# HGRN2 in a hybrid decoder trunk: the two pairs of heads in one run of small products

## The chip, the cores and the metric

The kernel runs on one core of one Trainium2 chip, in float32 throughout. The metric is device time in microseconds (us), as the median of several runs. One more execution was recorded with the hardware profiler; all rows of a profile come from such an execution.

## The reference

Two layers; in each a SwiGLU half step, three token mixers side by side on the same normalised input, an output projection, and another SwiGLU half step, on 512 tokens of width 1024. The change concerns one mixer, HGRN2: four heads of width 64, a gated linear recurrence, in chunks of 64 tokens.

```python
log_f = log_sigmoid(z) + log1p(lb * exp(-z))         # per token and channel
k = (1 - lb) * sigmoid(-z)

def step(state, inp):                                # one chunk of 64 tokens
    qb, kb, vb, lfb = inp
    bcum = cumsum(lfb, axis=-2)
    rel = bcum[..., :, None, :] - bcum[..., None, :, :]
    decay = where(causal, exp(where(causal, rel, 0)), 0)
    scores = einsum('bhtd,bhsd,bhtsd->bhts', qb, kb, decay)
    o = einsum('bhts,bhsv->bhtv', scores, vb) + einsum('bhtd,bhdv->bhtv', qb * exp(bcum), state)
    b_last = bcum[..., -1:, :]
    state = exp(b_last)[..., 0, :, None] * state + einsum('bhsd,bhsv->bhdv', kb * exp(b_last - bcum), vb)
    return state, o

o = rms_norm(o, out_gain) * silu(gate)
```

## The kernel before

Nearly all of the time goes into large dense products: 128x128 weights against 512 or 256 columns. Each float32 factor is split into a rounded part and a rest (ScalarE casts, VectorE subtracts, lines 435 and 438 for weights that come by DMA), and a product is three matmuls. A *granule* is one load of weight rows with its products; in the projections of the FoX mixer (`fox_qkv`, through `tokens`, line 536) a granule is 24 matmuls of 512 columns in four banks of the PSUM ("mm" three times and "po"), and its generator stops after each half, so that other work can be put between half granules of 12. Three such projections of four granules follow each other (first half of q and k, second half, v). When one is complete, ScalarE copies its four banks out (line 1696), and the next one uses the same banks.

HGRN2 works on two *pairs* of heads, two heads of 64 channels on the 128 partitions. `hgrn` is a generator, one for each pair, and stops at these places: after the decays; after the scaled keys; after their transposes (line 1426); after the state products U (line 1448), the scan over chunks and the operands of the first two levels; after each of four groups of score levels; after the outputs (lines 1577 and 1593); the end normalises.

The scores of a chunk, 64 by 64, are made level by level. Level n splits the chunk in blocks of 2^n tokens; within a block, queries of the second half meet keys of the first, with a decay relative to the middle. `operands(lev)` makes exp of the relative decay for keys and queries on VectorE and ScalarE (lines 1487, 1488, the exponential, 1495), `score(lev, ...)` multiplies on TensorE (line 1510 for levels 0 and 1, line 1518 for levels 2 to 6), `place` (lines 1530, 1535, 1538) takes the valid part from the bank into the matrix A under a mask. The groups are levels 0 and 1, 2 and 3, 4 and 5, and 6. All these products are small: 64x64 weights in a quarter of the array, with 32 or 64 columns, or 128x64 weights with 2 columns; each is recorded as two matmuls.

`mix` steps the two generators in turn and puts half granules of the dense projection behind each step, after the list `HGRN_BESIDE`: none behind the first steps of both, one behind each of the next six, two behind each of the next six, one behind each of the last two that have any. So on TensorE a run of small products of the first pair, dense work, a run of the second pair, dense work, and so on. `fox_decay` (line 1634) comes after the eighth step.

Dense products marked with `follow` keep the order in which they are written. The rest is ordered by the framework's scheduler when the program is built: by the order of the code, among what its own estimate of times takes to be ready; casts of weights have priority. Each engine then executes its queue in order. Temporary tiles of 128x512 come from a ring of ten (`tmp`). PSUM has eight banks: "mm" three, "sc" two, "pt" two, "po" one, each tag used in rotation; accesses to a bank by different engines are kept apart bank by bank. Before, U takes two "pt" banks for each pair, and the scores one or two "sc" banks for each pair and group.

Of the kernel before, what the change touches and what calls it, by code (L numbers as in the profile page):

```python
# [21 lines left out]
QUADS = ((("mm", 0), ("mm", 1), ("mm", 2), ("po", 0)), (("sc", 0), ("sc", 1), ("pt", 0), ("pt", 1)))  # L22

LEVELS = ((0, 1), (2, 3), (4, 5), (6,))
HGRN_BESIDE = (0, 0) + (1,) * 6 + (2,) * 6 + (1,) * 2

BESIDE = (3, 3, 1) + (1, 1, 1, 1, 1, 2, 2) + (1, 2, 2, 2, 2, 2, 1, 2, 2)
P = 128
T = 512
# [171 lines left out]
def halves(x):  # L201

    return x.rearrange("p (h t) -> p h t", h=2)
# [7 lines left out]
class Trunk:  # L211
# [944 lines left out]
    def mix(self, l, w, w_out, conv_w, out_gain, q_gain, k_gain, f_bias, next_gain, logits):  # L1156
# [3 lines left out]
        with tc.tile_pool(name=self.n("mix"), bufs=1) as mp:  # L1160
# [48 lines left out]
            with tc.tile_pool(name=self.n("hg"), bufs=1) as hp:  # L1209
                self.tt, self.tb = "t", 10  # L1210

                b, kb, q, S = (pair(mp, tag) for tag in ("b", "kb", "q", "S"))
                negc = mp.tile([NH, 2, T], F32R, tag="n", name=self.n("negc"))
                bz = features([(H_F, 256)], ("mm", "mm"), lambda: self.end_norm(self.bank("pt"), hp))
                if l == 0:
                    self.lower_bounds(logits, hp.tile([P, T], F32, tag="t", name=self.n("lb"), bufs=10))
                bg = features([(H_G, 256)], ("mm", "po"))
                inv = self.inv
                z, sg = pair(hp, "z"), pair(hp, "sg")
                for i in range(2):  # L1220
                    nc.vector.tensor_mul(halves(z[i]), unwoven(bz[i]), halves(inv))
                for i in range(2):
                    nc.vector.tensor_mul(halves(sg[i]), unwoven(bg[i]), halves(inv))
                self.table(SILU)
                for i in range(2):
                    self.act(sg[i], sg[i], AF.Silu)
                self.table(LNEXP)

                self.invc, self.inv2 = col("invc", 4), col("inv2", 4)
                row = self.dram.tile([1, T], F32, tag="row", name=self.n("row"))  # L1230
                nc.gpsimd.dma_start(row, inv[0:1, :])
                nc.gpsimd.dma_start(self.invc, row.rearrange("o (i p) -> (o p) i", p=P))
                nc.vector.scalar_tensor_tensor(
                    out=self.inv2, in0=self.invc, scalar=1.0 / HD, in1=self.invc,
                    op0=ALU.mult, op1=ALU.mult,
                )
                bq = features([(H_Q, 256)], ("mm", "mm"))
                for i in range(2):
                    nc.vector.tensor_mul(halves(q[i]), unwoven(bq[i]), halves(inv))

                bv = [self.bank(t) for t in ("mm", "sc", "sc", "po")]
                self.stream(
                    [(bv[i][:, :264], slice(0, 264), TOK[i]) for i in range(4)],
                    cols((H_I, 128), (F_F, 4), (H_I + 128, 128), (F_F + 4, 4)), self.xact, KD,
                )
                v = hp.tile([P, 4, 256], F32, tag="v", name=self.n("v"))
                zf = mp.tile([P, 4, NH], F32, tag="zf", name=self.n("zf"))
                for i in range(4):
                    nc.scalar.activation(
                        halves(v[:, i, :]), unwoven(bv[i][:, :256]), AF.Copy,  # L1250
                        scale=self.invc[:, i : i + 1],
                    )
                    nc.vector.scalar_tensor_tensor(  # L1253
                        out=halves(zf[:, i, :]), in0=unwoven(bv[i][:, 256:264]),
                        scalar=self.invc[:, i : i + 1], in1=halves(fb), op0=ALU.mult, op1=ALU.add,
                    )
                run = [
                    self.hgrn(l, pr, hp, z[pr], q[pr], v, sg[pr], og, S[pr], kb[pr], b[pr])
                    for pr in range(2)
                ]  # L1260
                half = []
                dense = self.fox_qkv(mp, hp, tokens, half)
                step = 0
                while run:
                    for g in list(run):
                        if next(g, "end") == "end":
                            run.remove(g)
                        step += 1
                        for _ in range(HGRN_BESIDE[step - 1] if step <= len(HGRN_BESIDE) else 0):
                            next(dense)  # L1270
                        if step == 8:
                            self.fox_decay(mp, hp, zf, negc)
            with tc.tile_pool(name=self.n("at"), bufs=1) as ap_:
                self.tt, self.tb = "t", 2
                attend = self.fox_attend(ap_, half, qkg)
# [101 lines left out]
        nc.vector.tensor_sub(self.yl[i], u, self.yh[i])  # L1377


    def hgrn(self, l, pr, hp, z, q, v, sg, og, S, kb, b):  # L1380

# [5 lines left out]
        tmp = lambda: hp.tile([P, T], F32, tag="t", name=self.n("t"), bufs=self.tb)  # L1389
        own = lambda tag, shape: hp.tile(shape, F32, tag=f"{tag}{pr}", name=self.n(tag))  # L1390
        lb, lb1 = self.lb[:, l, pr : pr + 1], self.lb1[:, l, pr : pr + 1]

        h, t, n = tmp(), tmp(), tmp()
        nc.vector.tensor_scalar(h, z, scalar1=0.0, scalar2=0.5, op0=ALU.min, op1=ALU.mult)
# [45 lines left out]

        U, dec, S = tmp(), tmp(), S.rearrange("p (v c) -> p v c", c=NCH)
        U3, dec3 = (a.rearrange("p (v c) -> p v c", c=NCH) for a in (U, dec))
        ub = [self.bank("pt") for _ in range(2)]
        for i in range(4):
            for par, hh in ((0, 0), (1, 1), (0, 1), (1, 0)):
                r = slice(CH * par, CH * par + CH)
                o = slice(64 * hh, 64 * hh + 64)
                nc.tensor.matmul(
                    ub[par][o, i * HD : (i + 1) * HD],
                    kt[r, i * P + 64 * hh : i * P + 64 * hh + 64],  # L1450
                    v[r, i, pr * P + 64 * hh : pr * P + 64 * hh + 64], start=True, stop=True,
                )
        for par in range(2):
            nc.scalar.copy(
                U3[:, :, par::2], ub[par][:, :256].rearrange("p (i v) -> p v i", i=4)
            )
# [14 lines left out]
        def operands(lev):  # L1471
            w, half = 2**lev // 2, halves(lev)
            e = tmp()
            if lev == 0:

                nc.vector.tensor_mul(e, q, k)
                return e
            if lev == 1:
                self.act(half(e, 1), half(lf, 1), AF.Exp)
                nc.vector.tensor_mul(half(e, 1), half(e, 1), half(q, 1))  # L1480
                nc.vector.tensor_mul(half(e, 0), half(e, 1), half(k, 0))
                return e
            n2 = T // (2 * w)
            ref = b.rearrange("p (n s) -> p n s", s=2 * w)[:, :, w - 1 : w].to_broadcast(
                [P, n2, w]
            )
            nc.vector.tensor_add(half(e, 0), half(kb, 0), ref)
            nc.vector.tensor_sub(half(e, 1), half(b, 1), ref)
            self.act(e, e, AF.Exp)
            if len(asked) % 2 == 0:  # L1490
                asked.append(tmp())
            else:
                asked.append(asked[-1])
            e2 = asked[-1][:, (len(asked) - 1) % 2 * (T // 2) :][:, : T // 2]
            nc.vector.tensor_mul(
                e2.rearrange("p (n w) -> p n w", w=w), half(e, 1), half(q, 1)
            )
            return e, e2


        asked = []

        def score(lev, e, sb, at):

            if lev > 1:
                e, e2 = e
            if lev < 2:
                for c in range(NCH):
                    r = slice(CH * (c % 2), CH * (c % 2) + CH)
                    nc.tensor.matmul(  # L1510
                        sb[0][r, 8 * at + c // 2 : 8 * at + 8 : 4], e[:, c * CH : (c + 1) * CH],
                        self.heads2, start=True, stop=True,
                    )
                return
            for i in range(4):
                for hh, par in ((0, 0), (1, 1), (0, 1), (1, 0)):
                    r, c = slice(64 * hh, 64 * hh + 64), 2 * i + par
                    nc.tensor.matmul(
                        sb[hh][CH * par : CH * par + CH, P * at + 32 * i : P * at + 32 * i + 32],
                        e[r, c * CH : (c + 1) * CH], e2[r, 32 * c : 32 * c + 32],  # L1520
                        start=True, stop=True,
                    )

# [23 lines left out]
        yield  # L1547
        for g, levels in enumerate(LEVELS):
            now, ready = ready, []
            asked.clear()  # L1550
            later = list(LEVELS[g + 1]) if g + 1 < len(LEVELS) else []
            sb = [self.bank("sc") for _ in range(2 if g else 1)]
            for at, lev in enumerate(levels):
                score(lev, now[at], sb, at)
            for at, lev in enumerate(levels):
                if later:
                    ready.append(operands(later.pop(0)))
# [441 lines left out]
```

## Time and profile before

| | |
|---|---|
| median of 3 runs | 1761.5 us (1760.98 to 1762.36) |
| the profiled execution, time | 1760.3 us |
| the profiled execution, span of the records | 1758.5 us |
| granted TensorE clock | 1.00 |
| TensorE matmuls busy | 1749.8 us, 13613 records |
| VectorE busy | 1410.7 us |
| ScalarE busy | 1009.7 us |

In the rows, PE is TensorE's matmuls, PEld its weight loads, DVE VectorE, ACT ScalarE, SP the engine that issues most DMAs. A row of a timeline has its start from the beginning of the span and its length, both in us, then engine, line, operation, output and inputs, shape and how many in a row; in brackets, idle time before it and what ended it. L451, L457, L458 and L536 are dense products.

### The profile page before, as it was taken

The numbers are of one execution on the slowest core, as the hardware profiler recorded it, in microseconds if no ns is written. First come the engines' busy times: TensorE is split into PE (matmuls) and PEld (weight loads), VectorE is DVE, ScalarE is ACT, GpSimd is POOL, SyncE is SP. The second block draws the span as 40 slices with busy tenths as digits, with TensorE's granted clock in tenths as the row PEclk, the third lists the DMA queues.
The fourth block names the chain that finished last, engine by engine and source line by source line (L and its number), as shares of the span: only waits on it lengthen the run. The fifth ranks groups of instructions, "written<-read, shape, count | busy, mean of one in ns | idle before, by whom it ended". The sixth has DMA issues, their size and how long they took to land.

```text
span 1758.5 us, 33346 instructions
## 1 busy us (share of the span) xinstructions
PE 1749.8 (100%) x13613; PEld 1644.2 (93%) x13613; DVE 1410.7 (80%) x1898; ACT 1009.7 (57%) x1397; POOL 177.2 (10%) x174
## 2 busy tenths in 40 slices
PE   9999999999999999999999999999999999999999
PEld 7999999888888899999989999998888889999998
DVE  7988788678777898888689887876778779888793
ACT  5565555465776565565446556555657655655652
POOL 0011120100000111112001111201000000120200
PEclk9999999999999999999999999999999999999999
DMA  7768784243543876868267787923435438687762
GB/s 203 187 144 198 181 178 110 73 125 88 138 119 98 214 169 155 204 168 172 84 187 168 178 185 175 190 76 79 120 95 141 115 109 215 156 180 192 162 139 96
DMA packets 257465, 262.34 MB, mean 149 GB/s; under 512 B 25832, under 2 KB 236528, under 8 KB 257312
## 3 DMA queue, kind: packets, MB, share of 16 engines
q1 hardware_dynamic: 201456, 192.02, 36.4%
q0 software_dynamic: 55840, 68.19, 24.1%
q8 instruction: 107, 1.75, 0.4%
q14 instruction: 46, 0.38, 0.1%
q10 hardware_dynamic: 16, 0.00, 0.0%
HBM read 226.15 MB, written 2.17 MB: 130 GB/s over the span
## 4 chain that ended last, share of the span: by engine, by line
PE 92%; DVE 5%; ACT 1%; issue 1%; DMA 1%; SPq 0%; ACTq 0%; DVEq 0%
PE mm L451 10%; PE mm L458 10%; PE mm L457 10%; PE mm L536 8%; PE sc L458 6%; PE sc L451 6%; PE sc L457 6%; PE pt L457 6%; PE pt L451 6%; PE pt L458 6%; PE po L451 3%; PE po L457 3%; PE po L458 3%; PE po L536 2%; PE sc L1767 1%; DVE hl L438 1%
## 5 line engine op out<-in xcount | busy, mean ns | idle before, releaser
L940 DVE TENSOR_TENSOR hl<-w,hl 128x1024 fp32r<-128x1024 f32 x279 | 340.7, 1223 | 90.1 <-ACT hl L938 88.4
L938 ACT CAST hl<-w 128x1024 fp32r<-128x1024 f32 x279 | 292.7, 1049 | 198.3 <-PE mm L458 56.0
L438 DVE TENSOR_TENSOR hl<-st,hl 128x1024 fp32r<-128x1024 f32 (+3 forms) x152 | 159.9, 1053 | 100.9 <-ACT hl L435 100.1
L435 ACT CAST hl<-st 128x1024 fp32r<-128x1024 f32 (+3 forms) x151 | 137.5, 911 | 158.2 <-PE po L458 44.4
L451 PE MATMUL mm<-xc,hl 128*128 128x256 f32 x698 | 191.6, 275 | 0.1
L458 PE MATMUL mm<-xc,hl 128*128 128x256 f32 x696 | 191.6, 275 | 0.0
L457 PE MATMUL mm<-xc,hl 128*128 128x256 f32 x696 | 191.5, 275 | 0.0
L451 PE MATMUL pt<-xc,hl 128*128 128x256 f32 x546 | 149.7, 275 | 0.0
L457 PE MATMUL pt<-xc,hl 128*128 128x256 f32 x544 | 149.7, 275 | 0.0
L458 PE MATMUL pt<-xc,hl 128*128 128x256 f32 x544 | 149.6, 275 | 0.0
L451 PEld LDWEIGHTS mm<-xc,hl 128*128 128x128 f32 x698 | 133.9, 192 | 0.3 <-ACT u L1058 0.3
L458 PEld LDWEIGHTS mm<-xc,hl 128*128 128x128 f32 x696 | 133.6, 192 | 0.4 <-DVE hl L940 0.4
L457 PEld LDWEIGHTS mm<-xc,hl 128*128 128x128 f32 x696 | 133.6, 192 | 0.0
L458 PE MATMUL sc<-xc,hl 128*128 128x256 f32 x464 | 127.8, 275 | 0.1
L451 PE MATMUL sc<-xc,hl 128*128 128x256 f32 (+1 forms) x466 | 127.7, 275 | 0.0
L457 PE MATMUL sc<-xc,hl 128*128 128x256 f32 x464 | 127.7, 275 | 0.0
L536 PE MATMUL mm<-hl,x 128*128 128x512 f32 x432 | 108.3, 386 | 0.4 <-DVE zf L1253 0.4
L451 PE MATMUL mm<-x,hl 128*128 128x512 f32 x272 | 105.4, 388 | 0.0
L451 PEld LDWEIGHTS pt<-xc,hl 128*128 128x128 f32 x546 | 104.7, 192 | 0.0
L457 PEld LDWEIGHTS pt<-xc,hl 128*128 128x128 f32 x544 | 104.4, 192 | 0.0
L458 PEld LDWEIGHTS pt<-xc,hl 128*128 128x128 f32 x544 | 104.4, 192 | 0.0
L458 PE MATMUL mm<-x,hl 128*128 128x512 f32 x272 | 103.1, 379 | 0.0
(524 smaller groups left out, 5454.6 us busy)
## 6 DMA issues: line engine op xcount, KB each, us to landing
w<-in_ffn_w_in_dram SPq DMA_DIRECT2D x124, 512.0 KB, 6.3
w<-in_ffn_w_out_dram POOLq DMA_DIRECT2D x50, 512.0 KB, 9.6
w<-in_ffn_w_out_dram SPq DMA_DIRECT2D x49, 512.0 KB, 4.7
st<-in_ffn_w_out_dram SPq DMA_DIRECT2D x39, 512.0 KB, 3.7
st<-in_w_mix_in_dram SPq DMA_DIRECT2D x72, 256.0 KB, 3.0
st<-in_ffn_w_in_dram SPq DMA_DIRECT2D x70, 256.0 KB, 3.9
w<-in_ffn_w_in_dram POOLq DMA_DIRECT2D x29, 512.0 KB, 10.0
w<-S POOLq DMA_DIRECT2D x29, 512.0 KB, 5.1
```

Source lines behind the costliest of these rows:

```text
L435: a = nc.scalar.copy(hi, src[:, c : c + w])
L438: b = nc.vector.tensor_sub(lo, src[:, c : c + w], hi)
L451: i = nc.tensor.matmul(acc[:, c], ah, bh[:, c.start // 2 : c.stop // 2, :], start=first and c.start == 0, stop=False, skip_group_check=True,)
L457: nc.tensor.matmul(acc, ah, bl, start=False, stop=False, skip_group_check=True)
L458: i = nc.tensor.matmul(acc, al, bh, start=False, stop=last, skip_group_check=True)
L536: self.follow("p", self.nc.tensor.matmul(acc, *((w, woven(x)) if toks is None else (x[:, toks], woven(w))), start=k == 0 and id(acc) not i ...
L938: A(nc.scalar.copy(hi, src))
L940: return lambda: V(nc.vector.tensor_sub(lo, src, hi))
L1767: mm = lambda *a, **k: E(nc.tensor.matmul(*a, skip_group_check=True, **k))
```

## The change

The two generators are stepped together from the U products on. Each has two more stops: after the U products, and after the score products of each group. So the small products of both pairs are issued one behind the other, then both pairs' evictions and next operands, then the half granules that stood behind each pair before: 2, 4, 4, 4 and 2. The first three steps alternate as before, with the same half granules; `fox_decay` comes after the first joint step.

The pairs share banks: a table `both` holds the banks of a group, and each pair has half of their 512 columns. The groups alternate between the "sc" and the "pt" banks.

The product of the relative decay with q is written in place, into the half of the operand tile that holds the queries' decay, instead of into a packed tile of its own (`e2`, `asked`); the score products read it there, in pieces of 2^(lev-1) columns.

```diff
-HGRN_BESIDE = (0, 0) + (1,) * 6 + (2,) * 6 + (1,) * 2
+HGRN_BESIDE = (0, 0, 1, 1, 1, 1), (2, 4, 4, 4, 2)
...
+                both = {}
                 run = [
-                    self.hgrn(l, pr, hp, z[pr], q[pr], v, sg[pr], og, S[pr], kb[pr], b[pr])
+                    self.hgrn(l, pr, hp, z[pr], q[pr], v, sg[pr], og, S[pr], kb[pr], b[pr], both)
                     for pr in range(2)
                 ]
...
-                step = 0
-                while run:
-                    for g in list(run):
-                        if next(g, "end") == "end":
-                            run.remove(g)
-                        step += 1
-                        for _ in range(HGRN_BESIDE[step - 1] if step <= len(HGRN_BESIDE) else 0):
-                            next(dense)
-                        if step == 8:
-                            self.fox_decay(mp, hp, zf, negc)
+                alone, together = HGRN_BESIDE
+                for step, n in enumerate(alone):
+                    next(run[step % 2])
+                    for _ in range(n):
+                        next(dense)
+                for step, n in enumerate(together):
+                    for g in run + run:
+                        next(g)
+                    for _ in range(n):
+                        next(dense)
+                    if step == 0:
+                        self.fox_decay(mp, hp, zf, negc)
+                for g in run:
+                    next(g)
+                for g in run:
+                    assert next(g, "end") == "end"
...
+        def shared(key, *tags):
+            if key not in both:
+                both[key] = [self.bank(tag) for tag in tags]
+            return [b[:, pr * T // 2 : (pr + 1) * T // 2] for b in both[key]]
...
-        ub = [self.bank("pt") for _ in range(2)]
+        ub = shared("u", "pt", "pt")
         for i in range(4):
...
+        yield
         for par in range(2):
             nc.scalar.copy(
...
-            if len(asked) % 2 == 0:
-                asked.append(tmp())
-            else:
-                asked.append(asked[-1])
-            e2 = asked[-1][:, (len(asked) - 1) % 2 * (T // 2) :][:, : T // 2]
-            nc.vector.tensor_mul(
-                e2.rearrange("p (n w) -> p n w", w=w), half(e, 1), half(q, 1)
-            )
-            return e, e2
+            nc.vector.tensor_mul(half(e, 1), half(e, 1), half(q, 1))
+            return e
...
+                    keys = e[r, c * CH : (c + 1) * CH]
+                    out = sb[hh][CH * par : CH * par + CH, P * at + 32 * i : P * at + 32 * i + 32]
                     nc.tensor.matmul(
-                        sb[hh][CH * par : CH * par + CH, P * at + 32 * i : P * at + 32 * i + 32],
-                        e[r, c * CH : (c + 1) * CH], e2[r, 32 * c : 32 * c + 32],
+                        out.rearrange("p (n w) -> p n w", w=2**lev // 2), keys, halves(lev)(keys, 1),
                         start=True, stop=True,
                     )
...
-            sb = [self.bank("sc") for _ in range(2 if g else 1)]
+            sb = shared(g, *(("pt", "sc")[g % 2 == 0],) * (2 if g else 1))
             for at, lev in enumerate(levels):
                 score(lev, now[at], sb, at)
+            yield
             for at, lev in enumerate(levels):
                 if later:
                     ready.append(operands(later.pop(0)))
```

More of the change, by code (lines that the diff above doesn't have):

```diff
@@ L1377, in conv_out, with hgrn @@
         nc.vector.tensor_sub(self.yl[i], u, self.yh[i])
-    def hgrn(self, l, pr, hp, z, q, v, sg, og, S, kb, b):
+    def hgrn(self, l, pr, hp, z, q, v, sg, og, S, kb, b, both):
         nc = self.nc
@@ L1489, in operands @@
             self.act(e, e, AF.Exp)
-            if len(asked) % 2 == 0:
-                asked.append(tmp())
-            else:
-                asked.append(asked[-1])
-            e2 = asked[-1][:, (len(asked) - 1) % 2 * (T // 2) :][:, : T // 2]
-            nc.vector.tensor_mul(
-                e2.rearrange("p (n w) -> p n w", w=w), half(e, 1), half(q, 1)
-            )
-            return e, e2
-        asked = []
+            nc.vector.tensor_mul(half(e, 1), half(e, 1), half(q, 1))
+            return e
         def score(lev, e, sb, at):
-            if lev > 1:
-                e, e2 = e
             if lev < 2:
@@ L1549, in hgrn @@
             now, ready = ready, []
-            asked.clear()
             later = list(LEVELS[g + 1]) if g + 1 < len(LEVELS) else []
-            sb = [self.bank("sc") for _ in range(2 if g else 1)]
+            sb = shared(g, *(("pt", "sc")[g % 2 == 0],) * (2 if g else 1))
             for at, lev in enumerate(levels):
                 score(lev, now[at], sb, at)
+            yield
             for at, lev in enumerate(levels):
```

## The prediction, made before the change was run

> **What bounds the kernel now.** I read the page first: the busy times, then the chain that ended last.
>
> ```profile
> PE 1749.8 (100%) x13613; PEld 1644.2 (93%) x13613; DVE 1410.7 (80%) x1898; ACT 1009.7 (57%) x1397; POOL 177.2 (10%) x174
> ...
> PE 92%; DVE 5%; ACT 1%; issue 1%; DMA 1%; SPq 0%; ACTq 0%; DVEq 0%
> ```
>
> TensorE (PE) works for the whole span and carries 92% of the chain, so time changes only by what happens on PE's own timeline. The change touches the HGRN2 part of each layer. The PE timeline places it, in the first layer, from the transposes near 381 us to the outputs that begin near 441 us; the second layer does the same about 868 us later. The windows view gives each engine's load there, for both layers, and then for two stretches of the first.
>
> ```profile
> 387.00:441.00 54.00, 54.00 (x654) 44.56 (x656) 44.19 (x97) 29.09 (x51) 1.04 (x2) 1.00 0.32 89
> 1255.00:1309.00 54.00, 54.00 (x651) 44.55 (x649) 44.26 (x97) 29.03 (x51) 1.04 (x2) 1.00 0.32 91
> ```
> ```profile
> 394.00:408.00 14.00, 14.00 (x121) 11.48 (x120) 12.78 (x24) 10.27 (x19) 0.00 (x0) 1.00 0.30 75
> 408.00:421.00 13.00, 13.00 (x178) 10.96 (x176) 12.90 (x35) 5.46 (x10) 0.52 (x1) 1.00 0.29 85
> ```
>
> After the stretch and its length come PE, weight loads, VectorE (DVE), ScalarE (ACT) and GpSimd, then the granted clock (1.00). The layers agree within 0.1 us on every engine, so I work out one and double it. PE has no hole. DVE is close behind it: 12.78 of 14 us, then 12.90 of 13. That is the second thing to watch: PE can only be brought forward as far as DVE delivers operands.
>
> What can be saved on a PE that is never idle? Only the turn between kinds of products, so the PE timeline comes next. Its columns are start, length of the group, and what it is. L536 is the dense stream (128x128 weights, 512 columns), L1518 the score products (64x64 weights, 32 columns). A product has two records.
>
> ```profile
> 412.04 1.46 PE L536 MATMUL mm<-hl,x 128*128 128x512 f32 x6
> 413.34 0.59 PE L536 MATMUL po<-hl,x 128*128 128x512 f32 x2
> ...
> 420.86 0.38 PE L536 MATMUL po<-hl,x 128*128 128x512 f32 x1
> 421.17 1.14 PE L1518 MATMUL sc<-t,t 64*64 64x32 f32 x64
> 422.23 3.72 PE L536 MATMUL mm<-hl,x 128*128 128x512 f32 x16
> 425.79 1.03 PE L536 MATMUL po<-hl,x 128*128 128x512 f32 x4
> ```
>
> Undisturbed, six dense records take 413.34 - 412.04 = 1.30 us, 0.217 each. The last dense record before the small run starts at 420.86 and its slot ends at 421.08; the next dense one starts at 422.23. So 64 small records hold the stream up for 1.15 us. The sixteen dense ones behind them take 425.79 - 422.23 = 3.56 us where 16 x 0.217 = 3.47 would do: another 0.09. A run of 64 costs 1.24 us in all. The last score level has runs of 32:
>
> ```profile
> 433.53 0.59 PE L536 MATMUL po<-hl,x 128*128 128x512 f32 x2
> 434.05 0.67 PE L1518 MATMUL sc<-t,t 64*64 64x32 f32 x32
> 434.65 1.56 PE L536 MATMUL mm<-hl,x 128*128 128x512 f32 x6
> ...
> 437.13 0.38 PE L536 MATMUL po<-hl,x 128*128 128x512 f32 x1
> 437.44 0.76 PE L1518 MATMUL sc<-t,t 64*64 64x32 f32 x32
> 438.13 1.56 PE L536 MATMUL mm<-hl,x 128*128 128x512 f32 x6
> ```
>
> The first: 434.65 - 433.53 - 2 x 0.217 = 0.69, with the 0.09 behind it 0.78. The second: 438.13 - 437.13 - 0.217 = 0.78, so 0.87. From 32 to 64 records the cost rises by 1.24 - 0.78 = 0.46 us; doing nothing but turning in and out costs 0.78 - 0.46 = **0.32 us per run**, however long the run. That is what the change goes after.
>
> **The change part by part.** *Pairs in one run.* Per layer the first pair's run and the second pair's become one, for the state products (U), the two lowest levels, levels 2 and 3, levels 4 and 5, and level 6. The outputs already follow each other without dense work between, and stay so. No product is added or removed, and the count of dense half granules is the same (20, with 2+4+4+4+2 behind the merged runs where it was 1+1, 2+2, 2+2, 2+2, 1+1). For the U and low-level runs the rows are:
>
> ```profile
> 387.27 0.69 PE L1448 MATMUL pt<-v,t 64*64 64x64 f32 x32
> ...
> 395.33 1.10 PE L1510 MATMUL sc<-heads,t 128*64 128x2 f32 x32
> ...
> 401.21 0.59 PE L536 MATMUL po<-hl,x 128*128 128x512 f32 x2
> 401.74 1.10 PE L1510 MATMUL sc<-heads,t 128*64 128x2 f32 x32
> 402.77 3.72 PE L536 MATMUL mm<-hl,x 128*128 128x512 f32 x16
> 406.36 1.13 PE L536 MATMUL po<-hl,x 128*128 128x512 f32 x4
> ```
>
> A U run of 32 lasts 0.69 against 0.67 for the score run of 32: I give it the same 0.32. The low-level run costs 402.77 - 401.21 - 2 x 0.217 + 0.09 = 1.22 us. The groups of the page's fifth part give one record's own time, 199 ns:
>
> ```profile
> L1510 PE MATMUL sc<-heads,t 128*64 128x2 f32 x128 | 4.4, 199 | 0.0
> ```
>
> So the 32 start within 1.10 - 0.20 = 0.90 us, 0.029 apart, 32 of them are 0.93 and the turn is 0.29. The merged level 6 is a run of 64: 1.24 instead of 0.78 + 0.87, a gain of 0.41; if the second run's extra 0.09 comes along, 0.32. Sum per layer: 0.32 + 0.29 + 0.32 + 0.32 + 0.41 = 1.66 us, twice 3.3 us; with the lower value for level 6, 3.2.
>
> *Operands in place.* The score products read their 32 moving columns straight out of the 64-column tile, in pieces of 2 to 32, where they read them closely packed. No row shows such a read. [...] The U row has 64 columns and takes 0.02 us more per 32 records than the 32-column row; 640 records (5 levels, 2 pairs, 16 products, 2 records, 2 layers) make 20 x 0.02 = 0.4 us. A gain has no row to speak for it: U shows that columns aren't what limits these runs. I take 0. [...]
>
> On DVE the product with q now lands strided and in place instead of packed. The nearest rows are these: L1481 writes strided in place, L1495 packed.
>
> ```profile
> 396.60 0.57 DVE L1481 TENSOR_TENSOR t<-t,lk 128x256 f32<-128x256 f32 x1
> ...
> 406.79 0.41 DVE L1495 TENSOR_TENSOR t<-t,q 128x256 f32<-128x256 f32 x1
> ```
>
> At most 0.16 us more for each of ten per layer, 1.6 us on DVE, not on PE's path as long as operands come early; at best nothing. I take nothing. One temporary tile less per stage loosens the ring of ten.
>
> *Shared banks.* Evictions of the first pair now wait for the second's products in the same bank, 0.93 us more. Queued behind them on DVE are the next levels' operands. Hidden: the next merged run comes four half granules later, 4 x 12 x 0.217 = 10.4 us.
>
> *The second pair earlier.* This is the price. Its level-1 operand is wanted three times 16 records after the run begins, at 395.33 - 0.32 = 395.01, plus 3 x 16 x 0.029 = 396.4; in the trace it was ready at 396.60 + 0.57 = 397.2. Its level-3 operand was ready at 406.79 + 0.41 = 407.2 and is wanted when the granules behind the low levels end, at 395.01 + 2 x 0.93 + 0.09 + 10.4 = 407.4 or a little later. The first is late by 0.8 us unless DVE reaches it sooner. I think it does: the ACT timeline shows what held the second pair back.
>
> ```profile
> 392.55 1.06 ACT L1564 COPY lk<-S 128x448 f32<-128x448 f32 x1 [2.47 <-DVE t L1481]
> 393.51 0.76 ACT L1454 COPY t<-pt 128x256 f32<-128x256 f32 x2
> ...
> 400.18 1.04 ACT L1696 COPY qk<-mm 128x512 f32<-128x512 f32 x2
> ...
> 405.20 0.63 ACT L341 ACTIVATE t<-t 128x512 f32<-128x512 f32 x1
> 405.73 0.57 ACT L1696 COPY qk<-po 128x512 f32<-128x512 f32 x1
> ```
>
> The second pair's U copies (393.51) stood behind a copy that waited 2.47 us for the first pair. With both U products done near 387.27 + 0.69 + 0.46 = 388.4 they need not, and the second scan, which followed them, can start some 2 us sooner. I cost the earlier pair at nothing, covered by those 2 us; without that cover it costs 0.8 us per layer.
>
> Against the profiled execution (1760.3 us, 1.2 below the median of 1761.5) the sum gives 1757.0; against the median, **1758.2 us**.
>
> **The rivals.** *Late second pair.* DVE, 98% busy, keeps its old times: PE waits 0.8 us at the low levels in each layer, the rest has margin. Gain 3.3 - 1.6 = 1.7: 1759.8 us. For it: the DVE load. Against it: the freed 2 us.
>
> *Not merged.* Instructions without a written order are placed by the framework's scheduler as they become ready. Where it sees the second pair's operands late, dense halves go in between and the runs stay apart: no gain, 1761.5 us. Against it: the old runs stayed whole, and from levels 2 and 3 on margins are microseconds.
>
> *The banks of the projection.* This is the slower one. Its four banks are reused at once by the next projection. So far the second pair's low-level run stood between (1.22 us); now nothing does. ACT empties them, in order. The first two copies began at 400.18, in front of the second pair's exponential of level 3 (405.20 to 405.83). Issued earlier in the code now, that exponential can come ahead of them in ACT's queue and hold them: first bank free at 405.83 + 0.52 = 406.35. PE wants it when the projection ends, at 401.21 + 2 x 0.217 + 0.93 - 0.32 = 402.3. It would stand for about 4.1 us per layer: 1761.5 - 3.3 + 8.2 = 1766.4 us. It turns the gain into a loss when the first copy ends after 402.3 + 1.66 = 404.0. Against it: the exponential itself would come sooner than 405.20, with its operands. [...] In this trace evacuation stays ahead of PE.
>
> **How the numbers follow.** Forecast (merged, no new wait) 0.56; late second pair 0.16; not merged 0.13; banks 0.12; the rest 0.03. The forecast's own spread is 1757.5 to 1758.9: the 0.4 us of strided reads, the level-6 term, and small waits that go or come. The range 1757.0 to 1762.0 takes in the second and third case with the scatter of the medians and leaves out the banks and the rest, about 0.15, and the tails. About what a measurement of this kernel can tell from no change is 0.2%, 3.5 us: the boundaries are 1758.0 and 1765.0. The forecast lies almost on the first, so a bit under half of it, with a little of the rest, counts as faster: 0.30. Slower is the bank case less its mild forms: 0.10. The same: 0.60.
>
> **What would show it.** In the new PE timeline: one run of 64 records for U, the low levels and level 6, 128 for the others, about 1.24 + 2 x 0.46 = 2.16 us of held-up stream for 128, and no gap but the turn. Wrong steps would show as: a dense group between two L1518 groups of one stage (not merged); the last quarter of L1510 starting late behind DVE (late pair); the second projection's first dense group late behind ACT L1696 (banks); L1518 records further apart than 0.46 / 32 = 0.0144 us (strided reads). The forecast is wrong if the turn isn't the fixed cost I read from runs of two lengths.

## The result, and the profile after

The changed kernel took 1757.95 us (median of 21 runs), the kernel before 1760.65 us (21 runs). The ratio is 0.9986, 95% interval 0.998 to 0.9993: by the ratio 2.5 us less, between 1.2 and 3.5. The interval lies below 1, so the kernel is faster, but by less than the 3.3 us of the sum; by the boundary of 0.2% that the prediction set, it counts as the same, the case to which it gave 0.60. The predicted 1758.2 us looks closer than it was: it started from 1761.5, a median of three runs, 0.85 us above the median of 21, and that hides that the gain came out smaller; the closeness is luck. One execution of the kernel before, beside e1 to e4 below, took 3022.98 us at a mean granted clock of 0.556; it is in no ratio here.

The profiled execution took 1757.89 us against 1760.3. The page's first lines:

```profile
span 1756.1 us, 33330 instructions
...
PE 1748.3 (100%) x13613; PEld 1645.5 (94%) x13613; DVE 1409.4 (80%) x1898; ACT 1010.5 (58%) x1397; POOL 177.0 (10%) x174
```

As many products as before, PE still full. The PE timeline of the first layer, at the places shown of before (U is now line 1461, the low levels 1512, the other levels 1522):

```profile
387.24 0.38 PE L536 MATMUL po<-hl,x 128*128 128x512 f32 x1
387.55 1.16 PE L1461 MATMUL pt<-v,t 64*64 64x64 f32 x64
388.64 1.56 PE L536 MATMUL mm<-hl,x 128*128 128x512 f32 x6
...
395.17 2.03 PE L1512 MATMUL sc<-heads,t 128*64 128x2 f32 x64
397.13 3.72 PE L536 MATMUL mm<-hl,x 128*128 128x512 f32 x16
...
402.42 3.68 PE L536 MATMUL mm<-hl,x 128*128 128x512 f32 x16
406.40 1.13 PE L536 MATMUL po<-hl,x 128*128 128x512 f32 x4 [0.30 <-ACT qk L1699]
407.37 0.59 PE L536 MATMUL mm<-hl,x 128*128 128x512 f32 x2
407.80 0.59 PE L536 MATMUL po<-hl,x 128*128 128x512 f32 x2
408.32 2.07 PE L1522 MATMUL pt<-t 64*64 64x32 f32 x128
410.32 1.56 PE L536 MATMUL mm<-hl,x 128*128 128x512 f32 x6
...
432.91 0.59 PE L536 MATMUL po<-hl,x 128*128 128x512 f32 x2
433.44 1.14 PE L1522 MATMUL pt<-t 64*64 64x32 f32 x64
434.50 1.56 PE L536 MATMUL mm<-hl,x 128*128 128x512 f32 x6
```

All five pairs of runs are merged (levels 4 and 5, not among the lines shown, have their 128 records from 420.88 on). A run of 128 holds the dense stream up for 410.32 - 407.80 - 2 x 0.217 = 2.09 us, 2.18 with what the dense records behind it lose. The same arithmetic on the starts of all dense records gives the gain by stage, per layer: U 0.36, low levels 0.38, levels 2 and 3 0.33, levels 4 and 5 0.33, level 6 0.42, together 1.81 us.

Not all of it was kept. Between 402.42 and 406.40 sixteen dense records of the second projection take 3.98 us instead of 3.47, and the four behind them 0.97 instead of 0.87: 0.61 us, 0.63 by the single records, where it was 0.14 before. The bracket names ScalarE's copy of a bank. So in the kernel before, too, emptying the banks was not quite ahead of PE.

To compare kernels I use one length per layer, the *stretch*: on the PE timeline, from the first dense record behind the first pair's transposes to the first one behind the outputs and the transposes that follow them. It holds the same products in every kernel here. Each kernel has one profile, so there are two values of it, one for each layer; in seven of the eleven profiles they agree within 0.04 us. Before it was 64.00 and 63.99 us, after 62.68 and 62.69: 1.31 per layer, as 1.81 less 0.49 of added wait would have it (1.32). Two layers make 2.6 us; the rest of the span accounts for 0.2 the other way.

The ScalarE timeline of the changed kernel shows why the copies are late (line 1699 copies a bank out, 1674 takes squares for the norms of q and k, 341 is an exponential, 435 a cast of weights):

```profile
400.56 0.64 ACT L1674 ACTIVATE fs<-qk 128x512 f32<-128x512 f32 x1
402.71 0.63 ACT L341 ACTIVATE t<-t 128x512 f32<-128x512 f32 x1 [1.51 <-DVE t L1502]
403.81 0.64 ACT L1674 ACTIVATE fs<-qk 128x512 f32<-128x512 f32 x1 [0.47 <-DVE fm L1675]
404.35 0.57 ACT L1699 COPY qk<-mm 128x512 f32<-128x512 f32 x1
404.81 1.05 ACT L435 CAST hl<-st 128x1024 fp32r<-128x1024 f32 x1
405.76 0.59 ACT L1699 COPY qk<-po 128x512 f32<-128x512 f32 x1
```

The projection ended at 402.42. The third bank's copy stands in the queue behind an exponential and a second square (line 1674), which both wait for VectorE; the fourth stands behind a cast of weights as well and ends at 406.35. PE stood until then.

### The profile page after: what moved, and what is told of

Same layout as the page of the kernel before. It is cut to its first block, busy times and chain, and to the rows that moved or that the text cites. A ratio compares the mean times of both kernels' runs of the same rounds, so it can differ in the third digit from the quotient of the medians.

```text
span 1756.1 us, 33330 instructions
## 1 busy us (share of the span) xinstructions
PE 1748.3 (100%) x13613; PEld 1645.5 (94%) x13613; DVE 1409.4 (80%) x1898; ACT 1010.5 (58%) x1397; POOL 177.0 (10%) x174
## 4 chain that ended last, share of the span: by engine, by line
PE 91%; DVE 5%; ACT 2%; issue 1%; DMA 1%; SPq 0%; ACTq 0%; DVEq 0%
PE mm L451 10%; PE mm L458 10%; PE mm L457 10%; PE mm L536 7%; PE sc L458 6%; PE sc L457 6%; PE sc L451 6%; PE pt L457 6%; PE pt L451 6%; PE pt L458 6%; PE po L457 3%; PE po L451 3%; PE po L458 3%; PE po L536 2%; PE sc L1770 1%; DVE hl L438 1%
```

## The experiments

All ran beside the kernel before; ratios are to it. The stretch is given for both layers. The last column counts executions whose mean granted clock, in thousandths, was below 1.000. The groups e1 to e4, e5 to e7, and e8 with e9 ran on three different chips, where the kernel before had medians of 1760.9, 1760.64 and 1760.76 us; its clocks in the last column are from these. The intervals reach some 1.5 us to each side, so smaller differences between two experiments are told by the stretch and not by the medians.

| kernel | median, us | ratio (95%) | stretch, us | clock below 1 |
|---|---|---|---|---|
| before | 1760.65 | | 64.00, 63.99 | 1 of 81 |
| changed | 1757.95 | 0.9986 (0.998 to 0.9993) | 62.68, 62.69 | 1 of 21 |
| e1 4,4,4,2,2 behind | 1757.7 | 0.9983 (0.9975 to 0.9992) | 62.05, 62.07 | 3 of 11 |
| e2 copies first | 1757.71 | 0.9981 (0.9972 to 0.999) | 63.74, 62.11 | 2 of 11 |
| e3 operands packed | 1756.86 | 0.9978 (0.9969 to 0.9987) | 62.08, 62.05 | 0 of 11 |
| e4 before, in place | 1762.09 | 1.0007 (0.9998 to 1.0016) | 64.71, 64.33 | 0 of 11 |
| e5 seven runs | 1758.39 | 0.9988 (0.9979 to 0.9997) | 62.72, 62.71 | 1 of 11 |
| e6 four runs | 1760.94 | 1.0004 (0.9995 to 1.0012) | 61.86, 65.60 | 11 of 11 |
| e7 e4, copies first | 1760.99 | 1.0 (0.9991 to 1.0009) | 63.83, 63.79 | 0 of 11 |
| e8 e1, decay early | 1756.93 | 0.9978 (0.9969 to 0.9987) | 62.26, 62.12 | 0 of 11 |
| e9 e8, packed | 1757.56 | 0.998 (0.9971 to 0.9989) | 62.26, 62.24 | 0 of 11 |

The theory to test: the gain is turns saved, and part is given back at the second projection's banks. The rival: strided operands make VectorE, and ScalarE behind it, slower.

**e1: the projections end where a small run begins.**

```diff
-HGRN_BESIDE = (0, 0, 1, 1, 1, 1), (2, 4, 4, 4, 2)
+HGRN_BESIDE = (0, 0, 1, 1, 1, 1), (4, 4, 4, 2, 2)
```

> Edit: the half granules behind the five joint runs are 4, 4, 4, 2, 2 instead of 2, 4, 4, 4, 2, so that one projection ends where a run of small products begins. Theory (turns saved, some given back at the projection's banks): the wait of the second projection's first granule for ScalarE's bank copies goes (0.07 + 0.46 + 0.10 us per layer in the changed kernel), because the low-level run of 64 records and the decay products (3.2 us) now stand between the two projections; about 1.2 us less than the changed kernel, 3.8 us less than the kernel before; every run keeps its length. Rival (the missing gain is a slower DVE because of strided operands, with ScalarE behind it): a wait appears at another place, the low levels or the outputs, and the time stays where the changed kernel is.

The wait is gone and the stretch is 0.63 us shorter per layer, as expected. Yet the median is only 0.25 us below the changed kernel's, not 1.2, and 3 of 11 executions had a clock below 1; that is taken up at e6. The clock is a part of it at most: the eight executions at 1.000 have a median of 1757.5, the changed kernel's twenty at 1.000 one of 1757.9. The rest is less than these medians can tell.

**e2: the bank copies first.**

```diff
-                nc.scalar.copy(
+                with self.tc.high_priority(): nc.scalar.copy(
                     qk[:, i].rearrange("p h w d -> p w h d"),
```

> Edit: the four copies that empty a projection's banks (q and k) get the scheduler's high priority, as weight casts have; nothing else. Theory: only ScalarE's order matters at the joint. The copy of the fourth bank goes ahead of a weight cast of 1.05 us, ends near 405.4 instead of 406.35 in the first layer, and the 0.57 us at the fourth bank goes; the 0.07 us at the third bank stays, since that copy still stands behind a square that waits for DVE. About 1.1 us less than the changed kernel. Rival (strided operands): nothing changes at the joint, or the delayed cast makes a dense product wait, and the time is the same or longer.

In the second layer only the third bank's 0.07 us is left: 62.11, as expected 0.6 less than in the changed kernel. ScalarE's order alone makes the wait. In the first layer of this profile the banks cost nothing, but that layer is no test: from 397 to 401 us the granted clock was 0.57 in the mean, which sets the dense stream back by 0.43 x 4.00 = 1.7 us and left ScalarE that much more time. The windows view has the granted clock (third from the end, behind GpSimd):

```profile
397.00:401.00 4.00, 4.00 (x23) 3.25 (x22) 3.80 (x8) 2.62 (x5) 0.00 (x0) 0.57 0.41 86
401.00:405.00 4.00, 4.00 (x20) 3.47 (x20) 4.00 (x10) 3.16 (x7) 0.00 (x0) 1.00 0.42 129
```

**e3: merged, operands packed again**, in the tile `e2` as before.

```diff
-            nc.vector.tensor_mul(half(e, 1), half(e, 1), half(q, 1))
-            return e
+            ...
+            nc.vector.tensor_mul(e2.rearrange("p (n w) -> p n w", w=w), half(e, 1), half(q, 1))
+            return e, e2
...
-                        out.rearrange("p (n w) -> p n w", w=2**lev // 2), keys, halves(lev)(keys, 1),
+                        out, keys, e2[r, 32 * c : 32 * c + 32],
```

> Edit: the changed kernel, but the queries' operand in a packed tile of its own again. Theory: the same time as the changed kernel within 0.3 us; the score records stay 14.6 ns apart, and the run of 128 records holds the dense stream up for 2.09 us either way. Rival (strided reads or writes cost): the runs get shorter, or DVE gets ahead and the wait at the second projection shrinks by 0.3 to 0.6 us per layer, and the time falls by 0.5 to 1.2 us.

Here my expectation failed, and the rival's size came out: the stretch is 0.6 us shorter, and the wait at the banks is 0.03 us. But it is not the rival's cause. The runs are no shorter, 2.09 us for 128 records both ways, and VectorE's product with q, mean of 20, takes 0.428 us in place (changed) and 0.426 packed (e3). So strided reads cost TensorE nothing here, strided writes cost VectorE nothing, and operands in place cost the banks' wait. On ScalarE:

```profile
402.46 0.63 ACT L341 ACTIVATE t<-t 128x512 f32<-128x512 f32 x1 [1.50 <-DVE t L1502]
403.00 0.61 ACT L1686 ACTIVATE fs<-qk 128x512 f32<-128x512 f32 x1
403.52 0.57 ACT L1711 COPY qk<-mm 128x512 f32<-128x512 f32 x1
403.99 1.05 ACT L435 CAST hl<-st 128x1024 fp32r<-128x1024 f32 x1
404.94 0.63 ACT L341 ACTIVATE t<-t 128x512 f32<-128x512 f32 x1
405.47 0.57 ACT L1711 COPY qk<-po 128x512 f32<-128x512 f32 x1
```

The same work in another order: one square ahead of the third copy instead of two, so no wait for VectorE's reduction there. The fourth bank is free at 406.04, in time.

**e4: the kernel before, with operands in place alone** (the edit of the operands in the diff, nothing else of it).

> Edit: the kernel before with one part of the change alone, the operands in place; pairs apart, banks not shared. Theory: the same time as the kernel before within 0.3 us, score runs of 64 records hold the stream up for 1.16 us as before. Rival (the gain comes from one temporary tile less and an earlier DVE, not from the turns): 1 us or more of the 2.5 us gain is already here.

Also not as I expected: the stretch is 0.71 and 0.34 us longer than before. The score runs are unchanged (1.16 us for 64); the loss is at the banks again, in the PE timeline the second group:

```profile
402.55 2.86 PE L536 MATMUL mm<-hl,x 128*128 128x512 f32 x12
405.94 1.13 PE L536 MATMUL mm<-hl,x 128*128 128x512 f32 x4 [0.53 <-ACT qk L1684]
```

Twelve records take 405.94 - 402.55 = 3.39 us instead of 2.60. In the first layer 0.2 us more went at the outputs. On ScalarE the cast stands ahead of both copies:

```profile
404.38 1.03 ACT L435 CAST hl<-st 128x1024 fp32r<-128x1024 f32 x1
405.31 0.58 ACT L1684 COPY qk<-mm 128x512 f32<-128x512 f32 x1
405.79 0.58 ACT L1684 COPY qk<-po 128x512 f32<-128x512 f32 x1
```

**e7: e4 with the copies first**, to tell order from strides.

> Edit: the kernel before with the operands in place, and the projection's bank copies with the scheduler's high priority. With operands in place alone the first dense group that needs the third bank stood 0.8 and 0.6 us in the two layers. Theory (in place costs only through ScalarE's order): the cast no longer stands ahead of the third and fourth copies, the wait shrinks to under 0.1 us, and the stretch is 64.0 us or less, as before. Rival (strided operands themselves cost): the stretch stays at 64.3 to 64.7 us.

```profile
404.27 0.57 ACT L1685 COPY qk<-mm 128x512 f32<-128x512 f32 x1
404.73 0.59 ACT L1685 COPY qk<-po 128x512 f32<-128x512 f32 x1
405.21 1.06 ACT L435 CAST hl<-st 128x1024 fp32r<-128x1024 f32 x1
```

With both copies ahead of the cast the wait is gone and the stretch is 0.2 us shorter than before. The kernel before with the copies first and packed operands was not run, but no wait is left in e7 for strides to cause. So operands in place cost through the order that the scheduler gives ScalarE. Why it gives another order (one temporary tile less, or other readiness) was not tried apart.

**e5: seven runs instead of five.**

```diff
-LEVELS = ((0, 1), (2, 3), (4, 5), (6,))
+LEVELS = ((0, 1), (2,), (3,), (4,), (5,), (6,))
-HGRN_BESIDE = (0, 0, 1, 1, 1, 1), (2, 4, 4, 4, 2)
+HGRN_BESIDE = (0, 0, 1, 1, 1, 1), (4, 4, 2, 2, 1, 1, 2)
```

> Edit: as in the run with 4, 4, 4, 2, 2 half granules behind, but levels 2, 3, 4 and 5 each have a run of their own, so seven joint runs instead of five, with 4, 4, 2, 2, 1, 1, 2 behind them; the same products and the same dense work. Theory (a run costs 0.33 us beyond its products, however long): each layer takes 0.66 us more than with five runs, 62.7 us instead of 62.05 from the second transposes to the end of the outputs, 1.3 us in all. Rival (the gain is from shared banks and an earlier second pair): no more than 0.2 us.

The stretch grew by 0.67 and 0.64 us over e1's, two turns of 0.33. (It is counted from the first transposes; "second" in the expectation was a slip.) The medians are 0.7 us apart where 1.3 was expected, within their intervals. The stretch confirms the fixed cost by adding it.

**e6: four runs.**

```diff
-HGRN_BESIDE = (0, 0, 1, 1, 1, 1), (2, 4, 4, 4, 2)
+HGRN_BESIDE = (0, 0, 1, 1, 1, 1), (4, 0, 8, 2, 2)
...
-                    if step == 0:
+                    if step == 2:
                         self.fox_decay(mp, hp, zf, negc)
```

> Edit: 4, 0, 8, 2, 2 half granules behind the joint runs, so that the low levels and levels 2 and 3 make one run of 192 records, and the decay products stand before levels 4 and 5. Theory: one turn less, 0.33 us per layer less than with five runs and no wait: 61.7 us for the stretch, 0.65 us in all, provided the second pair's level-3 operand is there some 4 us earlier than it had to be; where DVE is late with it, PE waits in the middle of the run and the gain is lost. Rival (turns don't matter): no difference or longer.

In the first layer this came out in part: 61.86 us, VectorE in time, but 0.2 less than e1 where 0.33 was expected. The low levels and the score products are of two kinds, and passing from one to the other seems to cost some 0.13 us of the turn; that is an estimate from this difference. The kernel as a whole was 3 us slower than e1. The second layer's PE timeline and windows:

```profile
1265.68 2.03 PE L1512 MATMUL sc<-heads,t 128*64 128x2 f32 x64
1267.64 3.04 PE L1522 MATMUL pt<-t 64*64 64x32 f32 x128
1271.58 4.65 PE L536 MATMUL mm<-hl,x 128*128 128x512 f32 x12 [0.90 <-PE pt L1522]
```
```profile
1262.00:1268.00 6.00, 6.00 (x106) 5.25 (x107) 5.82 (x15) 5.67 (x9) 0.00 (x0) 1.00 0.36 72
1268.00:1275.00 7.00, 6.10 (x127) 5.33 (x120) 7.00 (x18) 3.59 (x7) 0.00 (x0) 0.53 0.48 145
1275.00:1280.00 5.00, 5.00 (x24) 4.32 (x24) 4.93 (x16) 3.04 (x5) 0.52 (x1) 0.98 0.01 5
```

The granted clock was 1.00 up to 1268 and 0.53 in the mean of the 7.00 us behind it. It fell within the run, whose last 128 records took 3.04 us instead of 2.07, and the same products took 3.7 us more in this layer. All 11 executions had a mean clock below 1; where it fell, only the profiled one shows. Up to 1268 PE was busy (6.00 of 6.00 us in the first row of the windows), from 1265.68 on with small products, and the 0.90 us of idle time that the records show comes behind the run.

**e8 and e9: the decay products earlier**, behind the second pair's transposes, so that they don't add to the low levels' run; e9 with packed operands besides.

```diff
                     next(run[step % 2])
+                    if step == 5:
+                        self.fox_decay(mp, hp, zf, negc)
...
-                    if step == 0:
-                        self.fox_decay(mp, hp, zf, negc)
```

> Edit: 4, 4, 4, 2, 2 half granules behind the joint runs, and the decay products behind the second pair's transposes instead of ahead of the low levels. With 4, 4, 4, 2, 2 the decay products and the merged low levels made 3.2 us without dense work, and 3 of 11 executions had a granted clock of 0.999, with 192 records in one run (4.06 us) all of 11 were at 0.999 or less. Theory (a long stretch of small products makes the throttle halve the clock for some us behind it): the longest stretch is now 2.2 us beside the outputs, no execution shows a clock under 1.000, the slow executions near 1759.5 go, and the median falls by 0.5 to 1 us; the stretch on the PE timeline stays at 62.0 to 62.2 us per layer. Rival (the clock dips come at random): about as many executions below 1.000 as before.

> Edit: as the run before, with the queries' operand in a packed tile again. Theory (where no wait is left, packed or in place is the same): the same as that run within 0.3 us; these two are the fastest, near 1756.7 us, 4 us below the kernel before. Rival (in place costs by itself): this one is 0.5 us or more below the run before.

e8's longest time without dense work, beside the outputs, is 2.09 us, and no execution of either kernel was below 1.000, as the theory has it. e8's median is 0.8 us below e1's, 0.6 against the kernel before on each chip; the two intervals overlap. e8's first layer has 0.15 us of wait at the banks again, which its second has not. e9 was not below e8 but 0.6 above, with a stretch of 0.1 at most between them; that difference I can't place, and it is within the intervals. e3 and e8, at 0.9978, are the best here: nearly 4 us below the kernel before, about 1 us below the changed one, though their intervals overlap with its.

## Why the prediction was right and wrong

*The turn* was right. Two lengths of run in the old trace gave 0.32 us; e5 and the merged runs gave 0.33. U (0.36) and the low levels (0.38 instead of 0.29) brought more: the decay products ahead of the low levels no longer begin 0.07 us late behind the second pair's U copies (0.29 us after the start of the last dense record before, 0.22 after).

*The late second pair* did not come, for the reason given: its U copies are no longer held up and begin at 390.37 instead of 393.51. Its level-1 operand was ready at 394.86 + 0.46 = 395.3, before 396.4, and the run of 64 low-level records has no gap.

```profile
390.37 0.87 ACT L1468 COPY t<-pt 128x256 f32<-128x256 f32 x2
...
394.86 0.46 DVE L1495 TENSOR_TENSOR t<-t,lk 128x256 f32<-128x256 f32 x1
```

*Not merged* did not come. *Operands in place* is the step that failed: "I take 0" was right for the reads and writes, as e3 shows, and wrong for the kernel, since the edit moved ScalarE's order: 0.6 us per layer between the changed kernel and e3. That a strided read could cost what 64 columns cost, the 0.4 us in the forecast's spread, no run shows: runs of 128 records hold the dense stream up for 2.09 us strided (changed) and packed (e3). I had priced instructions and not the queue they stand in.

*The banks* I made a rival with 4.1 us per layer at the first bank. The mechanism came true at the third and fourth bank, at 0.49 us more than before. Between the all-or-nothing cases lay the one that happened; the forecast's spread ("small waits that go or come") was too narrow a place for it. Sum: 1.81 - 0.49 = 1.32 per layer instead of 1.66; measured 1.31. So the turns, with the earlier decay products, brought 0.15 more than predicted and the banks took 0.49: two errors that partly cancel.

*The clock* was in no rival. For the changed kernel it matters little, 1 of 21 executions.

## What to carry to other kernels

With TensorE full, as here, what small products cost beyond their number is the turn in and out of them (0.33 us a run in e5); two run lengths in a trace give it, and fewer, longer runs save it. After such a regrouping look at what the old interleaving had covered, here the emptying of banks between two projections, and at the order of the engine that does it. Watch how long a merged run keeps dense work away: in these runs the clock held with up to 2.4 us and sometimes fell with 3.2, and one fall cost 1.7 or 3.7 us where five turns save 1.8.

## What the runs showed of the hardware that I had not expected

The granted clock fell more often the longer small products kept dense work away. By the longest time without dense work (beside the outputs): up to 2.4 us, none of the 44 executions of e4, e7, e8 and e9 was below 1.000, and of 81 of the kernel before only the one named with the result; at 3.2 us (changed, e1, e2, e3, e5), 7 of 65; at 4.06 us (e6), 11 of 11. A spell cost 1.7 us in e2's profile and 3.7 us in e6's. The outputs keep the dense stream away for 4.65 to 4.85 us in every kernel, but 2.1 of them are four products with 128x128 weights and 512 columns, and the profiles show no fall there. What makes it fall, and why 3.2 us sometimes suffices, is open.

The score records come 14.6 ns apart whether their 32 columns are packed or strided, and U's records with 64 columns nearly as close (0.943 us from the first to the last of 64, 15.0 ns apart): in these runs neither the number of columns nor their layout is the limit.
